# Two row blocks of the modulation weights per visit, accumulated in PSUM, in a two-layer DiT kernel

## Chip, core and metric

The kernel runs on one core of a Trainium2 chip. The metric is device time in microseconds (us) of one execution, start to end. TensorE is called PE, its weight loads PEld, VectorE DVE, ScalarE ACT, GpSimd POOL, and SP is the engine from whose queue nearly all loads are issued.

## The reference

Two layers of a diffusion transformer act on 512 latent tokens (stream `l`) and 256 context tokens (stream `c`) of width 1024. Each layer starts from six modulation rows per stream, which are one matrix product of a single vector with a wide weight matrix; the change concerns this product alone.

```python
silu_c = jax.nn.silu(c)
silu_cc = jax.nn.silu(c_ctx)
for l in range(DEPTH):
    mod_l = (silu_c @ w_mod[l] + b_mod[l])[:, None, :]       # w_mod[l]: 1024 x 6144
    mod_c = (silu_cc @ w_mod[l] + b_mod[l])[None, None, :]
    sh1, sc1, g1, sh2, sc2, g2 = jnp.split(mod_l, 6, axis=-1)
    h_l = modulate(rms_norm(x, norm1_g[l]), sh1, sc1)
    y_l, y_c = token_mixer(h_l, h_c, w_in[l], ...)           # projections, retention, attention, w_out
    x = x + g1 * y_l
    h_l = modulate(rms_norm(x, norm2_g[l]), sh2, sc2)
    x = x + g2 * expert_choice_ffn(h_l, ...)                 # 16 experts, top-k tokens
```

All arithmetic is float32; the projections split each operand into a high and a low part and add three products.

## The kernel before

**Stages.** Layer 0 first forms the modulation columns that it needs at once (`mod_half`), then projects both streams through `w_in` (some 50 to 410 us of the profile), multiplies by `w_out`, selects tokens and runs the experts, whose weights stream through a ring of 2 MB buffers (to about 1045 us). Layer 1 repeats this.

**Projections.** `proj` makes one projection of 256 output columns in eight steps (row blocks of 128). A tile `wraw` (512 KB) holds the weights of four steps, so a projection has two loads (L359), one before step 1 and one before step 5. Every two steps ACT copies half of `wraw` into `wH` (L275) and DVE or POOL subtracts to get `wL` (L276); there are two buffers of each. Then come 18 matmuls per step into `acc`: L354 and L355 read `wH`, L356 reads `wL`.

**Modulation.** `mod_gen` walks over 2048 columns at a time, row block by row block. One visit for one row block loads two tiles `wm` of 512 KB (L197), does four matmuls of 32 columns of weights side by side on PE (L201, one for each quarter of PSUM tile `ps_mod`), and DVE adds `ps_mod` to the running sum `modt` (L203). There are 40 visits in the stage: 16 for layer 0 and 24, made ahead, for layer 1.

**One set of buffers.** `wraw`, `wm` and later `wraw_o` (the weights of `w_out`, L866) share four buffers under the tag `wraw` (`NW = 4`). They are handed out in rotation, so a load may start when the tile four places earlier in the order of allocation has been read for the last time. SP issues its loads in order: behind one that waits, all wait.

**Order.** `weave` runs a projection step by step and after every step advances the attention by 0.8, the retention by 1.0 and the modulation by `M0R = 0.6` visits; after the last projection the rate of the modulation is `M1R = 0.5`. The counter starts anew with every projection, so visits come after steps 2, 4, 5 and 7. Within such an order the program's scheduler may move instructions of one engine past each other where their data allow it; on the chip each engine then works strictly in the order written.

Of the kernel before, what the change touches and what calls it, by code (L numbers as in the profile page):

```python
# [22 lines left out]
F32 = mybir.dt.float32  # L23
# [33 lines left out]
M0R, M1R = 0.6, 0.5  # L57
ATR, RTR, RTR2 = (0.8, 0.85), (1.0, 1.0), 0.7
# [12 lines left out]
def weave(main, *fills):  # L71

    acc = [0.0] * len(fills)
    for _ in main:
        for i, (g, r) in enumerate(fills):
            acc[i] += r
            while acc[i] >= 1.0:
                acc[i] -= 1.0
                next(g, None)
    return  # L80
# [9 lines left out]
def kernel(ctx_stack: ExitStack, tc: tile.TileContext, x, c, ctx, c_ctx, w_mod, b_mod, norm1_g,  # L90
# [4 lines left out]
    PE, ACT, DVE, POOL, SP = nc.tensor, nc.scalar, nc.vector, nc.gpsimd, nc.sync  # L95
# [50 lines left out]
    cT = cst.tile([128, KC, 32], F32, name="cT")  # L146
# [39 lines left out]
    def mod_gen(l, wp, pp, groups):  # L186

        for b in groups:
            m = wp.tile([128, 512], F32, name="modt", tag="modt", bufs=2)
            POOL.memset(m, 0.0)  # L190
            for r in range(2):
                POOL.dma_start(m[r:128:32], b_mod[l, 2048 * b:2048 * b + 2048].rearrange("(q n) -> q n", n=512))
            for k in range(KC):
                w = []
                for h in range(2):
                    w.append(wp.tile([128, 2, 512], F32, name="wm", tag="wraw", bufs=NW))
                    SP.dma_start(w[h], w_mod[l, 128 * k:128 * k + 128, 2048 * b + 1024 * h:2048 * b + 1024 * h + 1024]  # L197
                                 .rearrange("p (q n) -> p q n", q=2))
                ps = pp.tile([128, 512], F32, name="ps_mod", tag="t", bufs=4)
                for q in range(4):  # L200
                    PE.matmul(ps[32 * q:32 * q + 32], cT[:, k, :], w[q // 2][:, q % 2, :], start=True, stop=True,  # L201
                              tile_position=(0, 32 * q))
                DVE.tensor_add(m, m, ps)  # L203
                if k == KC - 1:
                    if b:
                        for r in range(2):
                            POOL.dma_start(mod_d[l][b][r].rearrange("(q n) -> q n", n=512), m[r:128:32])
                    mod_cols(l, b, m, pp)
                yield

    def mod_half(wp, pp, hf):

        m = wp.tile([128, 512], F32, name="modt", tag="modt", bufs=2)
        POOL.memset(m, 0.0)
        for r in range(2):
            POOL.dma_start(m[r:64:32], b_mod[0, 0:2048].rearrange("(q n) -> q n", q=2)[:, 512 * hf:512 * hf + 512])
        for k in range(0, KC, 2):
            ps = pp.tile([128, 512], F32, name="ps_mod", tag="t", bufs=4)
            for i in range(2):
                w = wp.tile([128, 2, 512], F32, name="wm", tag="wraw", bufs=NW)  # L220
                SP.dma_start(w, w_mod[0, 128 * (k + i):128 * (k + i) + 128, 0:2048]
                             .rearrange("p (q n) -> p q n", q=2)[:, :, 512 * hf:512 * hf + 512])
                for q in range(2):
                    g = 32 * (2 * i + q)
                    PE.matmul(ps[g:g + 32], cT[:, k + i, :], w[:, q, :], start=True, stop=True, tile_position=(0, g))
            DVE.tensor_add(m, m, ps)
            if k < KC - 2:
                yield
        ps = pp.tile([128, 4, 4, 32], F32, name="ps_mc", tag="t", bufs=4)
        for j in range(4):  # L230
            PE.transpose(ps[:, j].rearrange("p q r -> p (q r)"), m[:, 128 * j:128 * j + 128], ident)
        cs = slice(4 * hf, 4 * hf + 4)
        tmp = m[:, 0:32].rearrange("p (q s r) -> p q s r", q=4, r=2)
        DVE.tensor_copy(tmp, ps[:, :, :, 0:2].rearrange("p s q r -> p q s r"))
        DVE.tensor_tensor(tmp[:, 0:2], tmp[:, 0:2], tmp[:, 2:4], OP.add)
        for r in range(2):
            DVE.tensor_copy(B1[0][r][:, cs], tmp[:, 0, :, r])
            DVE.scalar_tensor_tensor(A1[0][r][:, cs], tmp[:, 1, :, r], 1.0, n1col[0][:, cs], op0=OP.add, op1=OP.mult)
        yield

    def mod_cols(l, b, m, pp):
        ps = pp.tile([128, 4, 4, 32], F32, name="ps_mc", tag="t", bufs=4)
        for s in range(4):
            PE.transpose(ps[:, s].rearrange("p q r -> p (q r)"), m[:, s::4] if b else m[:, 128 * s:128 * s + 128], ident)
        for r in range(2):
            v = ps[:, :, :, r].rearrange("p s q -> p q s")

            def o(t):
                return t[l][r].rearrange("p (q s) -> p q s", q=2)

            def g(t):
                return t[l].rearrange("p (q s) -> p q s", q=2)
            if b == 0:
                DVE.tensor_copy(o(B1), v[:, 0:2])
                DVE.scalar_tensor_tensor(o(A1), v[:, 2:4], 1.0, g(n1col), op0=OP.add, op1=OP.mult)
            elif b == 1:
                DVE.tensor_copy(o(B2), v[:, 2:4])
            else:
                DVE.scalar_tensor_tensor(o(A2), v[:, 0:2], 1.0, g(n2col), op0=OP.add, op1=OP.mult)
# [701 lines left out]
    def router_cols(l, streams, pp, R):  # L961

        for s in streams:
            ri = RI[s]
            R.wrA[s] = rp.tile([128, KC, 32], F32, name="wrA" + s)
            POOL.memset(R.wrA[s], 0.0)
            POOL.tensor_tensor(R.wrA[s][:, :, :16], R.wr, A2[l][ri][:, :, None].to_broadcast([128, KC, 16]), OP.mult)
            ps = pp.tile([128, 512], F32, name="ps_r", tag="t", bufs=4)[:, :16]
            for j in range(KC):
                PE.matmul(ps, B2[l][ri][:, j:j + 1].to_broadcast([128, 128]), R.wr[:, j, :], start=(j == 0),  # L970
                          stop=(j == KC - 1))
            R.bB[s] = rp.tile([128, 16], F32, name="bB" + s)
            DVE.tensor_copy(R.bB[s], ps)
            yield
# [539 lines left out]
    for l in range(2):  # L1514
# [3 lines left out]
        if True:  # L1518
# [18 lines left out]
            with ExitStack() as s2:  # L1537
                pp = s2.enter_context(tc.tile_pool(name=f"pp{l}", bufs=1, space=PSUM))
                m0 = router_cols(l, streams, pp, R) if l else None
                if l == 0:  # L1540
# [10 lines left out]
                    ps = pp.tile([128, 512], F32, name="ps_t", tag="t", bufs=4)  # L1551
# [8 lines left out]
                    m0 = mod_half(wq, pp, 0)  # L1560
# [11 lines left out]
                    m0 = chain(mod_gen(0, wq, pp, range(1, 3)), router_cols(0, streams, pp, R), mod_gen(1, wq, pp, range(0, 3)))  # L1572
# [11 lines left out]
                pj = projections(l, p, wq, pp, S, st, need)  # L1584
# [26 lines left out]
                with ExitStack() as s3:  # L1611
                    w = s3.enter_context(tc.tile_pool(name=f"mx{l}", bufs=1, side="left"))
                    Sp = w.tile([128, 6, 2, 2, 64], F32, name="Sp")

                    def ret_all():
                        while "rv" not in ready:
                            yield
                        for s in "cl":
                            yield from ret_states(s, p, pp, S[s], T, Sp)
                        ready.add("states")  # L1620
                        while not {"rq", "g0", "g1"} <= ready:
                            yield
                        for s in reversed(streams):
                            yield from ret_gen(s, w, p, pp, S[s], T, Sp)

                    at = attn_all(streams, w, p, pp, S, T, ready, st)
                    rt = ret_all()
                    runs.update(at0=at, states=rt)
                    for n in ORDER[l:]:
                        ss = "lc" if two or n in ("rk", "rv") else "l"  # L1630
                        weave(pj[n](ss), (at, ATR[l]), (rt, RTR[l]), (m0, M0R))
                        later.append(lambda n=n: ready.add(n))
                        if l and n == "rv":
                            ring.load(N0)
                    while later:
                        later.pop(0)()
                    weave(at, (rt, RTR2), (m0, M1R))
                    drain(rt, m0)
            p_s.close()
            ml_s, po_s, pc_s = ExitStack(), ExitStack(), ExitStack()  # L1640
# [40 lines left out]
            with ExitStack() as s2:  # L1681
                if not two:
                    p = po_s.enter_context(tc.tile_pool(name=f"po{l}", bufs=1, side="left"))
                pp = s2.enter_context(tc.tile_pool(name=f"pq{l}", bufs=1, space=PSUM))
# [134 lines left out]
            with ExitStack() as s2:  # L1819
                pp = s2.enter_context(tc.tile_pool(name=f"pe{l}", bufs=1, space=PSUM))  # L1820
# [85 lines left out]
```

## Time and profile before

| What | Value |
|---|---|
| median of 3 runs | 1892.11 us (1891.56 to 1894.91) |
| profiled execution, its own time | 1889.7 us |
| its span in the profile | 1887.9 us |
| PE busy | 1770.4 us (94%) |
| DVE, ACT, POOL busy | 655.8, 479.8, 329.9 us |
| issue to landing, median: `wm`, `wraw`, `wraw_o` | 4.6, 3.9, 4.1 us |

The span is 1.8 us shorter than that execution's own time. Busy means that at least one instruction of the engine was under way. PE is busy nearly all the time in the projections and in the experts, so a microsecond in which PE stands still there is a microsecond of the run unless something later makes up for it.

### The profile page before, as it was taken

Reading aid. Unit: us, or ns where it says so; the run is one execution under the profiler, and the core shown is the slowest. Engines: PE = TensorE matmul, PEld = TensorE weight load, DVE = VectorE, ACT = ScalarE, POOL = GpSimd, SP = SyncE. Lnnn points to the kernel's source line nnn. Section 1 sums busy time; section 2 is a strip of 40 time slices with the busy share of each in tenths; the row PEclk is TensorE's granted clock in tenths of the full one; section 3 lists DMA queues with packets and bytes.
Section 4 is the critical chain, followed back from the end, with each engine's and each line's share of the span. In section 5 each row is a group of like instructions: output and inputs, shape, how many; then the busy total and the mean of one; then the engine's idle time right before and its main releaser. Section 6 shows DMA issues by size and latency. Waiting matters only on the chain. (4 is left out here: it accounts for less than half of the span.)

```text
span 1887.9 us, 30047 instructions
## 1 busy us (share of the span) xinstructions
PE 1770.4 (94%) x12581; PEld 1018.5 (54%) x12581; DVE 655.8 (35%) x1671; ACT 479.8 (25%) x960; POOL 329.9 (17%) x341
## 2 busy tenths in 40 slices
PE   5899999999899999999999789899959999999995
PEld 2788877767533333333333688877745444534442
DVE  5645435673621001110001755446341122221224
ACT  3435434353411001010000446454331000000001
POOL 3323123333201011011001333322410000000001
PEclk9999999999899999999999899999979999999998
DMA  8454354257789999999998411111747999999995
GB/s 278 155 191 157 106 202 151 90 186 279 300 340 408 414 401 401 423 400 399 395 412 325 169 43 37 57 34 38 297 185 291 420 430 429 429 429 428 431 428 206
DMA packets 88919, 528.42 MB, mean 280 GB/s; under 512 B 9352, under 2 KB 31932, under 8 KB 64720
## 3 DMA queue, kind: packets, MB, share of 16 engines
q1 hardware_dynamic: 83040, 511.24, 68.0%
q0 software_dynamic: 5744, 15.26, 2.9%
q8 instruction: 99, 1.62, 0.3%
q14 instruction: 36, 0.29, 0.0%
HBM read 510.41 MB, written 16.06 MB: 279 GB/s over the span
## 5 line engine op out<-in xcount | busy, mean ns | idle before, releaser
L1133 PE MATMUL ps_g<-ring,xTl 128*32 128x512 f32 (+1 forms) x1472 | 238.0, 596 | 4.2 <-DMA ring<-in_w_gate_dram 3.0
L1133 PE MATMUL ps_u<-ring,xTl 128*32 128x512 f32 (+1 forms) x1536 | 233.1, 592 | 3.1 <-DMA ring<-in_w_up_dram 2.4
L1133 PE MATMUL ps_d<-ring,aT 128*32 128x512 f32 (+1 forms) x1536 | 234.6, 593 | 0.3 <-ACT sil L1241 0.3
L1270 ACT ACTIVATE aT<-ps_t 128x512 f32<-128x512 f32 x16 | 9.6, 598 | 619.0 <-PE ps_t L1266 578.1
L354 PE MATMUL acc<-wH,hHl 128*128 128x256 f32 x512 | 153.8, 301 | 2.7 <-ACT hHl L343 1.2
L1133 PEld LDWEIGHTS ps_g<-ring,xTl 128*32 128x32 f32 (+1 forms) x1472 | 72.7, 121 | 154.1 <-issue 137.5
L1133 PEld LDWEIGHTS ps_u<-ring,xTl 128*32 128x32 f32 (+1 forms) x1536 | 69.9, 119 | 153.1 <-issue 146.0
L355 PE MATMUL acc<-wH,hLl 128*128 128x256 f32 x512 | 147.0, 287 | 3.5 <-DVE hLl L344 3.4
L356 PE MATMUL acc<-wL,hHl 128*128 128x256 f32 x512 | 147.1, 287 | 1.1 <-DVE wL L276 1.1
L1133 PEld LDWEIGHTS ps_d<-ring,aT 128*32 128x32 f32 (+1 forms) x1536 | 70.4, 119 | 142.5 <-issue 136.7
L354 PEld LDWEIGHTS acc<-wH,hHl 128*128 128x128 f32 x512 | 99.7, 195 | 30.3 <-issue 23.7
L276 POOL TENSOR_TENSOR wL<-wraw,wH 128x512 fp32r<-128x512 f32 x44 | 57.5, 1308 | 275.0 <-ACT wH L275 263.8
L355 PEld LDWEIGHTS acc<-wH,hLl 128*128 128x128 f32 x512 | 99.8, 195 | 4.4 <-DVE hLl L344 4.4
L356 PEld LDWEIGHTS acc<-wL,hHl 128*128 128x128 f32 x512 | 99.8, 195 | 4.0 <-DVE wL L276 2.4
L1268 DVE COPY aT<-ps_t 128x512 f32<-128x512 f32 x16 | 11.1, 692 | 253.2 <-PE ps_t L1266 253.2
L1249 DVE TENSOR_TENSOR sil<-ps_u,sil 128x512 f32<-128x512 f32 x32 | 22.1, 692 | 220.8 <-PE ps_u L1133 220.8
L1185 POOL TENSOR_TENSOR x<-z,xTl 128x512 f32<-128x512 f32 x3 | 5.1, 1717 | 493.4 <-DVE x L1187 493.4
L678 DVE TENSOR_REDUCE mc<-ps_s 128x1 f32<-128x513 f32 (+2 forms) x80 | 55.2, 690 | 83.3 <-PE ps_s L675 52.1
L275 ACT ACTIVATE wH<-wraw 128x512 fp32r<-128x512 f32 x88 | 55.1, 629 | 95.6 <-PE acc L355 44.9
L680 ACT ACTIVATE P<-ps_s,mc 128x513 f32<-128x513 f32 (+2 forms) x80 | 55.1, 689 | 94.5 <-DVE mc L678 94.5
L1123 PE MATMUL ps_x<-OT,xn 128*128 128x128 f32 x512 | 67.0, 297 | 8.1 <-DVE OT L1115 8.1
L1123 PEld LDWEIGHTS ps_x<-OT,xn 128*128 128x128 f32 x512 | 65.3, 210 | 10.0 <-DVE OT L1115 8.5
(491 smaller groups left out, 3172.0 us busy)
## 6 DMA issues: line engine op xcount, KB each, us to landing
ring<-in_w_up_dram SPq DMA_DIRECT2D x62, 2048.0 KB, 16.6
ring<-in_w_gate_dram SPq DMA_DIRECT2D x61, 2048.0 KB, 13.3
ring<-in_w_down_dram SPq DMA_DIRECT2D x61, 2048.0 KB, 17.0
wm<-in_w_mod_dram SPq DMA_DIRECT2D x96, 512.0 KB, 4.6
wraw<-in_w_in_dram SPq DMA_DIRECT2D x44, 512.0 KB, 3.9
wraw_o<-in_w_out_dram SPq DMA_DIRECT2D x24, 512.0 KB, 4.1
ring<-in_w_gate_dram SPq DMA_DIRECT2D x12, 512.0 KB, 4.8
ring<-in_w_down_dram SPq DMA_DIRECT2D x12, 512.0 KB, 15.6
```

The costliest lines, as they stand in the source:

```text
L275: ACT.activation(H, src, AF.Copy)
L276: sub_eng().tensor_sub(L, src, f32(H))
L354: PE.matmul(ps, aH, bH, start=start, stop=False)
L355: PE.matmul(ps, aL, bH, start=False, stop=False)
L356: PE.matmul(ps, aH, bL, start=False, stop=stop)
L678: DVE.tensor_reduce(mc[:, 0:1], sc, AX.X, OP.max, negate=True)
L680: ACT.activation(P[:, :nk + 1], sc, AF.Exp, bias=mc[:, 0:1], accum_out=mc[:, 1:2])
L1123: PE.matmul(ps[:, j], R.xn[:, t, c0:c0 + 128], OT[:, t], start=(t == 0), stop=(t == 3))
L1133: PE.matmul(G[h][c:c + n], lhs[:, k, c:c + n], W[e][:, j, 512 * h:512 * h + 512], start=(k == 0), stop=(k == KC - 1), tile_position=(0, c))
L1249: DVE.tensor_mul(sil[p][:, hs], U[h], sil[p][:, hs])
L1268: DVE.tensor_copy(aT[p][:, 4 * h:4 * h + 4], ps)
L1270: ACT.activation(aT[p][:, 4 * h:4 * h + 4], ps, AF.Copy)
```

## The change

A visit now covers two row blocks: it loads four tiles `wm`, does eight matmuls, of which the second four are added to the first in PSUM, and DVE makes one addition. The rates of the modulation in `weave` are halved, so that as many row blocks are done per projection step; by the counter, visits now come after steps 4 and 7 of a projection.

```diff
             for k in range(KC):
                 w = []
+                if k % 2 == 0:
+                    ps = pp.tile([128, 512], F32, name="ps_mod", tag="t", bufs=4)
+                    both = []
                 for h in range(2):
                     w.append(wp.tile([128, 2, 512], F32, name="wm", tag="wraw", bufs=NW))
                     SP.dma_start(w[h], w_mod[l, 128 * k:128 * k + 128, 2048 * b + 1024 * h:2048 * b + 1024 * h + 1024]
                                  .rearrange("p (q n) -> p q n", q=2))
-                ps = pp.tile([128, 512], F32, name="ps_mod", tag="t", bufs=4)
-                for q in range(4):
-                    PE.matmul(ps[32 * q:32 * q + 32], cT[:, k, :], w[q // 2][:, q % 2, :], start=True, stop=True,
-                              tile_position=(0, 32 * q))
+                both.append(w)
+                if k % 2 == 0:
+                    continue
+                for i in range(2):
+                    for q in range(4):
+                        PE.matmul(ps[32 * q:32 * q + 32], cT[:, k - 1 + i, :], both[i][q // 2][:, q % 2, :],
+                                  start=i == 0, stop=i == 1, tile_position=(0, 32 * q))
                 DVE.tensor_add(m, m, ps)
...
-                        weave(pj[n](ss), (at, ATR[l]), (rt, RTR[l]), (m0, M0R))
+                        weave(pj[n](ss), (at, ATR[l]), (rt, RTR[l]), (m0, M0R / 2))
...
-                    weave(at, (rt, RTR2), (m0, M1R))
+                    weave(at, (rt, RTR2), (m0, M1R / 2))
```

**In the middle of a projection.** The first place is the queue of SP around `wraw_934` of before, the second load of the first projection with visits; in the change this load is `wraw_932`. This is SP before:

```order
L359 DMA wraw_793<-in_w_in_dram 128x4x256
L197 DMA wm_852<-in_w_mod_dram 128x1024
L197 DMA wm_854<-in_w_mod_dram 128x1024
L197 DMA wm_924<-in_w_mod_dram 128x1024
L197 DMA wm_926<-in_w_mod_dram 128x1024
L359 DMA wraw_934<-in_w_in_dram 128x4x256
```

And this is SP in the change, with the line numbers of the changed file:

```order
L365 DMA wraw_793<-in_w_in_dram 128x4x256
L200 DMA wm_915<-in_w_mod_dram 128x1024
L200 DMA wm_917<-in_w_mod_dram 128x1024
L200 DMA wm_919<-in_w_mod_dram 128x1024
L200 DMA wm_921<-in_w_mod_dram 128x1024
L365 DMA wraw_932<-in_w_in_dram 128x4x256
```

The order of the loads is the same in both; in both the second `wraw` takes the buffer of the first of the four `wm` ahead of it (852, and now 915).

PE at the same place before: the visit that reads `wm_924` and `wm_926`, and then step 5 of the projection, whose `wH_936` and `wL_937` are made from `wraw_934`. The visit that reads `wm_852` stands two steps earlier.

```order
L562 MATMUL ps_t_919<-ident_66,kl_709 128x128 x2
L201 MATMUL ps_mod_928<-wm_924,cT_106 32x512 x2
L201 MATMUL ps_mod_928<-wm_926,cT_106 32x512 x2
L354 MATMUL acc_799<-wH_936,hHl_350 128x256
L355 MATMUL acc_799<-wH_936,hLl_351 128x256
L356 MATMUL acc_799<-wL_937,hHl_350 128x256
```

PE there in the change (`wH_934` and `wL_935` are made from `wraw_932`):

```order
L568 MATMUL ps_t_905<-ident_66,kl_709 128x128 x2
L207 MATMUL ps_mod_914<-wm_915,cT_106 32x512 x2
L207 MATMUL ps_mod_914<-wm_917,cT_106 32x512 x2
L207 MATMUL ps_mod_914<-wm_919,cT_106 32x512 x2
L207 MATMUL ps_mod_914<-wm_921,cT_106 32x512 x2
L360 MATMUL acc_799<-wH_934,hHl_350 128x256
L361 MATMUL acc_799<-wH_934,hLl_351 128x256
L360 MATMUL acc_812<-wH_934,hHc_352 128x256
L362 MATMUL acc_799<-wL_935,hHl_350 128x256
```

The visit that frees the buffer of the load has moved from two steps ahead of its use to directly ahead of it.

**At the end of the stage.** The second place is SP where the last `wm` are followed by the first loads of `w_out` (`wraw_o`), a modulation row (`g1`) and the residual (`x`, 2 MB). Before:

```order
L197 DMA wm_4514<-in_w_mod_dram 128x1024
L197 DMA wm_4516<-in_w_mod_dram 128x1024
L197 DMA wm_4559<-in_w_mod_dram 128x1024
L197 DMA wm_4561<-in_w_mod_dram 128x1024
L866 DMA wraw_o_4636<-in_w_out_dram 128x2x512
L866 DMA wraw_o_4689<-in_w_out_dram 128x2x512
```

And in the change:

```order
L200 DMA wm_4537<-in_w_mod_dram 128x1024
L200 DMA wm_4539<-in_w_mod_dram 128x1024
L200 DMA wm_4541<-in_w_mod_dram 128x1024
L200 DMA wm_4543<-in_w_mod_dram 128x1024
L872 DMA wraw_o_4596<-in_w_out_dram 128x2x512
L270 DMA g1_4582<-mod01_109 128x1024
L1704 DMA x_4583<-in_x_dram 128x2x1024 x2
L872 DMA wraw_o_4649<-in_w_out_dram 128x2x512
```

On PE the last visit, which reads `wm_4537` to `wm_4543`, now stands behind the last matmuls of the attention and directly ahead of the `w_out` product; the first `wraw_o` takes the buffer of `wm_4537`, and `g1` and `x` have moved ahead of the second `wraw_o`.

## Rows read from the trace of the kernel before

**Rows 1.** The head of the page: the profiled span.

```profile
span 1887.9 us, 30047 instructions
```

**Rows 2.** Busy time by stretch: PE, PEld, DVE, ACT, POOL, clock, DMA share, GB/s.

```profile
100.00:400.00 300.00, 298.73 (x2254) 234.46 (x2253) 154.94 (x438) 124.26 (x256) 81.28 (x89) 1.00 0.45 150
600.00:1000.00 400.00, 397.99 (x3668) 130.48 (x3664) 43.01 (x73) 26.05 (x58) 41.99 (x31) 1.00 1.01 404
```

**Rows 3.** Instructions on tile ps_mod: count, duration min/median/max in ns.

```profile
L203 DVE TENSOR_TENSOR modt<-modt,ps_mod x40: 674/687/690, 76.4 to 407.3; 128x512 f32<-128x512 f32 x40
```

**Rows 4.** Timeline of PE around one visit: start us, us, instruction.

```profile
84.85 0.28 PE L356 MATMUL acc<-wL,hHc 128*128 128x256 f32 x1
85.06 1.07 PE L201 MATMUL ps_mod<-wm,cT 128*32 128x512 f32 x8
86.06 0.39 PE L354 MATMUL acc<-wH,hHl 128*128 128x256 f32 x1
86.28 0.28 PE L355 MATMUL acc<-wH,hLl 128*128 128x256 f32 x1
86.40 0.28 PE L356 MATMUL acc<-wL,hHl 128*128 128x256 f32 x1
```

**Rows 5.** Timeline of SP, 84 to 143 us: three issues of projection weights.

```profile
86.16 0.38 SPq L359 DMA_DIRECT2D wraw<-in_w_in_dram  x1
...
124.13 0.38 SPq L359 DMA_DIRECT2D wraw<-in_w_in_dram  x1
...
138.40 0.38 SPq L359 DMA_DIRECT2D wraw<-in_w_in_dram  x1
```

**Rows 6.** Timeline of ACT: the splits that waited for these three loads.

```profile
90.53 0.63 ACT L275 ACTIVATE wH<-wraw 128x512 fp32r<-128x512 f32 x1 [2.32 <-DMA wraw<-in_w_in_dram]
...
127.99 0.63 ACT L275 ACTIVATE wH<-wraw 128x512 fp32r<-128x512 f32 x1 [0.49 <-DMA wraw<-in_w_in_dram]
...
142.39 0.64 ACT L275 ACTIVATE wH<-wraw 128x512 fp32r<-128x512 f32 x1 [0.40 <-DMA wraw<-in_w_in_dram]
```

**Rows 7.** Instructions on tile wraw, and its loads from issue to landing.

```profile
L276 POOL TENSOR_TENSOR wL<-wraw,wH x44: 1263/1291/1594, 34.5 to 1318.3; 128x512 fp32r<-128x512 f32 x44
L276 DVE TENSOR_TENSOR wL<-wraw,wH x44: 675/692/1608, 36.0 to 1313.3; 128x512 fp32r<-128x512 f32 x44
...
DMA to landing us min/median/max: 3.5/3.9/6.8
```

**Rows 8.** Tile wm: its loads from issue to landing.

```profile
DMA to landing us min/median/max: 3.5/4.6/5.8
```

**Rows 9.** Waits of the SP queue, 71 to 413 us, the longest in total.

```profile
SPq L359 <- PE ps_mod L201: 107.3, 18, 12.3
```

**Rows 10.** Timeline of PE where the stage ends.

```profile
406.12 1.07 PE L201 MATMUL ps_mod<-wm,cT 128*32 128x512 f32 x8
...
408.85 1.15 PE L698 MATMUL ps_t<-ident,P 128*128 128x128 f32 x8
409.92 1.08 PE L711 MATMUL ps_o<-PT,avc 128*64 128x256 f32 x8
410.84 1.03 PE L711 MATMUL ps_o<-PT,avl 128*64 128x256 f32 x8
412.87 0.50 PE L354 MATMUL acc<-wH,mHl 128*128 128x512 f32 x1 [1.00 <-ACT mHl L275]
```

**Rows 11.** Timeline of SP there.

```profile
403.88 7.67 SPq L866 DMA_DIRECT2D wraw_o<-in_w_out_dram  x5
```

**Rows 12.** PE busy, granted clock, DMA share and GB/s around pauses of PE.

```profile
1201.60:1204.36 2.76, 0.73 (x6) 1.00 0.57 188
1204.36:1207.77 3.41, 3.12 (x16) 0.50 0.00 0
...
1827.50:1829.90 2.40, 0.01 (x2) 1.00 0.99 423
1829.90:1833.30 3.40, 3.40 (x16) 1.00 0.97 414
```

## The prediction

> **What bounds it now.** I began with the busy shares by stretch. From 100 to 400 us, in which most of the 40 visits lie, PE is busy 298.73 of 300 us, DVE 154.94, ACT 124.26, POOL 81.28, and the DMA engines 45% [rows 1, 2]: the stage is bound by the row of work on PE. So one addition less per pair on DVE gives nothing by itself; 20 additions of 0.687 us, 13.7 us [rows 3], go from an engine that is idle half the time. Behind this stage come the experts, where PE and the DMA engines are both full (share 1.01, 404 GB/s) [rows 2]; their transfers start only after it, so what the stage loses or gains reaches the end of the run in full.
>
> Next I looked at what the PE work waits for. The queue of SP waited 18 times, 107.3 us in all, for `ps_mod` before a projection load could start [rows 9]: the visits free the buffers of the projection weights. The visit that begins at 85.06 is followed by the issue at 86.16, 1.1 later [rows 4, 5]; this distance is 1.07 to 1.09 for all 18. The load issued at 86.16 is split by ACT from 90.53, those of 124.13 and 138.40 from 127.99 and 142.39: 4.37, 3.86 and 3.99, mean 4.07, and in all three ACT was waiting for the load [rows 5, 6]. The split takes 0.63, the subtraction on DVE 0.69 [rows 6, 7]. So, counted from the start of the visit that frees the buffer, `wH` is ready at 1.1 + 4.07 + 0.63 + some 0.07 for two hand-overs = 5.87 us, and `wL` 0.73 later, at 6.60. Before, every such load has another whole visit and at least one step of 18 matmuls between the two, and PE hardly ever waits.
>
> **The change, part by part.**
>
> *Work of PE.* The eight matmuls of a pair do the same passes as twice four. Removed is one entry into the narrow weights and one exit per pair. Between 84.85 and 85.06 lie 0.21 instead of the 0.12 that such a matmul takes (86.28 to 86.40), and the first matmul behind the visit takes 0.22 instead of 0.12 (86.06 to 86.28) [rows 4]: 0.09 + 0.10, times 20 visits saved, is 3.8, say -4 us. The visit itself lasts 1.0 (85.06 to 86.06), a double one 2.0. The Trainium skill, "TensorEngine Tiling (Array Packing)", Key Properties, says that changing the tiling mode drains TensorE; the trace agrees, with these 0.1 us on either side.
>
> *The loads of projection weights.* This is where the change costs. In the order of SP nothing moves, and each `wraw` still takes the buffer of the first `wm` ahead of it. But that `wm` now belongs to a visit four tiles long which stands directly ahead of the step that needs the load (after step 4), or one step ahead (after step 7). So the wait of [rows 9] ends a whole visit later, and the 5.87 us must be covered by the double visit (2.0) and by what the new order puts between it and the first use. I took the order of PE in the changed kernel, and priced what stands between: 0.12 per matmul of 256 columns [rows 4], 0.13 per transpose, 0.12 per value product [rows 10]. For the place shown above it is nothing: 2.0 us of cover for 5.87, and 2.35 for the 6.60 of `wL`, so PE stands still for 4.25. There are 19 such loads; two, beside the router's two turns without visits, have 18 us of cover and more. For the other 17, in order, cover up to the first use of `wH`: 2.0, 4.1, 2.5, 4.8, 2.7, 5.2, 4.2, 5.8, 2.0, 4.1, 4.9, 5.5, 4.1, 5.4, 4.9, 6.1, 4.9. The stall is the greater of 5.87 less this and 6.60 less the cover of `wL`: 4.3, 1.8, 3.7, 1.0, 3.4, 0.7, 1.8, 0.1, 4.1, 1.8, 1.2, 0.4, 2.2, 0.5, 1.1, 0.4, 1.2. Sum: **29.7 us**. What is queued behind the waiting matmul is all of PE, the attention included; ACT waits at its split, with the attention's exponentials behind it.
>
> The bounds: with the quickest landing, 3.5 against the median 3.9 [rows 7], every stall is 0.4 shorter, some 6 less (24). With landings of 4.6, as the `wm` loads have when several run at once [rows 8], it is 0.7 more each, 41. I take the middle since three other loads follow the load at once in both kernels.
>
> *The fourth `wm` of a visit after step 7* takes the buffer of the `wraw` loaded in mid-projection. It starts after the second half is split, POOL's 1.29 included [rows 7], and lands 4.6 later [rows 8]: 1.1 + 4.07 + 0.63 + 0.63 + 1.29 + 0.3 + 4.6 = 12.6 after the earlier visit began, 13 to 14 where POOL or ACT is held up. The shortest distance in the order is 9.8 of work plus the stall of 3.4 to 4.3, plus 1.5 inside the visit: 14 to 15. I take +1, between 0 and 5.
>
> *The end of the stage.* Before, the last visit starts at 406.12, the first `wraw_o` is issued at 403.88, and PE loses only 1.00 ahead of the `w_out` product [rows 10, 11]. In the change the last two visits have 18 transposes and value products between them (2.3 us), and the four loads of the last wait for the one before: first landing 1.1 + 4.6 after its start, the fourth later by three times 512 KB at the 404 GB/s of [rows 2], 3.9: some 3.4 of stall. Then the first `wraw_o` waits for the last visit (5.87 against 2.0 plus the addition and four transposes): 1 to 2 us, in place of the 1.00. And `g1` and `x`, 2.5 MB or 6 us of transfer, now stand ahead of the second `wraw_o`: up to 2. Together **+6**, between +2 and +9.
>
> *The clock.* A pause of PE has a second price. From 1201.60 to 1204.36 PE was busy 0.73 of 2.76 us, and for the next 3.41 us the granted clock was 0.50, the 1.2 GHz level: 1.7 us lost. After an idle 1827.50 to 1829.90 it stayed 1.00 [rows 12]. I went through all pauses of PE in the timeline: of the six over 2 us five were followed by the low clock, of those from 1.3 to 1.9 some one in three. Of my stalls five are over 2 us, three are 1.8, one or two lie at the end: 7 or 8 falls of 1.7 to 2, **+13**, between 0 and +22.
>
> *Layer 1* has only the router's columns on this rate; they move from step 2 to step 4: nothing, hidden by PE's own work.
>
> **Sum.** -4 + 29.7 + 1 + 6 + 13 = +45.7. The profiled execution took 1889.7, which gives 1935.4; the median of the runs is 2.4 above it, so on that scale about **1937**.
>
> **Rivals.**
>
> 1. *The stalls come, but the clock holds*, as after 1829.90: +33, 1925. Against it: five of six.
> 2. *The loads land later* than the mean, because a projection load and three `wm` now start within 1.5 us of each other, or ACT, held at its splits, delays the attention which I counted as cover. Landings of 6.8, the longest [rows 7], are 2.9 over the median; on 12 of the 17 loads that is 35 more: 1960 and above. For it: landing times do spread from 3.5 to 6.8; against it: the load is first in its queue.
> 3. *The loads are hidden anyway*, within 0.2% (3.8 us, about what a measurement of this kernel can tell from no change): the order finds cover. Against it: it is written out, and twelve of the 17 places have under 5 us of cover. The Trainium skill, "Perfetto Trace Analysis", Identifying Performance Opportunities, reads a gap that repeats on the engine that should be full as a sign of too few buffers; this trace shows no such gap yet, and by that rule the change would make one.
> 4. *Faster.* The deciding point is a cover of 5.87 us at each use. If the split could start 4 us sooner (the buffer free before the visit), only the removed entries and exits remain, -4, and at most the 13.7 of DVE where it stands on the path: 1874 to 1888. For it: DVE's work shrinks; against it: [rows 9] say that the buffer is what is waited for.
>
> **Chances.** The forecast, stalls with falls of the clock (1929 to 1950): 0.60. Rival 1 or a smaller sum (1912 to 1929): 0.20. Rival 2 (1950 and above): 0.15. Rival 3: 0.02. Rival 4: 0.03. The low end is -4 + 24 + 0 + 2 + 0 = +22, 1914; the high end -4 + 41 + 3 + 8 + 20 = +68, 1960. Between them lie more than 8 in 10. Slower by over 0.2%: 0.95, within 0.2%: 0.02, faster: 0.03.
>
> **What would show it.** In the profile after, from 70 to 420 us: waits of PE or its weight loads at L360 or L362 for ACT's `wH` or DVE's `wL`, some 25 to 40 us in all, three to four of about 4 us where the visit is followed at once by step 5; ACT waiting longer for `wraw` than before; PE below 90% busy where it was 99.6%; granted clock below 1.00 in some of the 50 us stretches; the first `w_out` matmul at about 458 instead of 412.87; 20 additions in place of 40; and after that stage everything as before, only later. I am wrong if the loads are issued other than 1.1 us after their visit, if they land in much less than 4, or if PE pauses at other work.

## The result, and the profile after the change

The change made the kernel slower: 1956.13 us median (1952.9 to 1957.71, 4 runs) against 1891.84 of the kernel before on the same chip (1888.8 to 1894.91, 4 runs). The ratio is 1.0341, 95% interval 1.0325 to 1.0358. I had forecast 1937, in a range from 1914 to 1960: the direction is right and the place for the most part, the size is 19 us short.

The profiled execution took 1955.45 us. The first thing to settle is where the 65.8 us between the two profiled times were lost. The first rows here are the first projection matmul, before and after (timelines of PE; columns are start, duration, instruction, and in brackets the idle time ahead and what ended it):

```profile
33.94 0.38 PE L354 MATMUL acc<-wH,hHl 128*128 128x256 f32 x1 [1.20 <-ACT wH L275]
```

```profile
36.82 0.39 PE L360 MATMUL acc<-wH,hHl 128*128 128x256 f32 x1 [1.20 <-ACT wH L281]
```

The next view of the kernel after the change is the timeline of PE where the stage ends, which answers to [rows 10]:

```profile
469.12 2.00 PE L207 MATMUL ps_mod<-wm,cT 128*32 128x512 f32 x8
471.50 1.05 PE L207 MATMUL ps_mod<-wm,cT 128*32 128x512 f32 x4 [0.38 <-DMA wm<-in_w_mod_dram]
472.79 1.05 PE L207 MATMUL ps_mod<-wm,cT 128*32 128x512 f32 x4 [0.23 <-DMA wm<-in_w_mod_dram]
475.59 0.75 PE L250 MATMUL ps_mc<-ident,modt 128*128 128x128 f32 x4 [1.75 <-DVE modt L209]
477.05 0.47 PE L360 MATMUL acc<-wH,mHl 128*128 128x512 f32 x1 [0.70 <-DVE A21c L265]
```

The first `w_out` matmul moved from 412.87 [rows 10] to 477.05, 64.2 later, so nearly all of the loss lies ahead of it. Of this, 2.9 lie ahead of the projections, where the change touches nothing; in the executions profiled below this start lies between 33.7 and 37.8 whatever the kernel. From the first projection matmul to the first `w_out` matmul it was 378.93 before and is 440.23 now: +61.3. These are the busy times by stretch, first that whole stretch of before, and then of the kernel after the change the same stretch, the two stretches of [rows 2], and three pieces of 50 us (columns: from and to, length, busy time of PE, PEld, DVE, ACT and POOL with the number of instructions, granted clock, DMA share, GB/s):

```profile
33.94:412.87 378.93, 369.93 (x2792) 291.19 (x2792) 206.04 (x565) 160.01 (x337) 104.14 (x117) 0.99 0.46 154
```

```profile
36.82:477.05 440.23, 394.31 (x2793) 311.30 (x2793) 200.07 (x551) 165.80 (x355) 107.28 (x122) 0.94 0.38 131
100.00:400.00 300.00, 274.32 (x2031) 222.15 (x2024) 119.43 (x334) 110.94 (x233) 70.61 (x77) 0.97 0.39 136
600.00:1000.00 400.00, 397.86 (x3656) 132.95 (x3652) 47.08 (x86) 33.71 (x75) 39.53 (x31) 1.00 1.00 406
...
100.00:150.00 50.00, 42.57 (x322) 37.04 (x315) 19.27 (x55) 16.75 (x41) 13.14 (x14) 0.93 0.45 159
200.00:250.00 50.00, 49.63 (x411) 42.25 (x411) 21.24 (x56) 24.12 (x43) 9.09 (x11) 1.00 0.23 76
400.00:450.00 50.00, 46.52 (x255) 34.03 (x257) 27.54 (x90) 14.61 (x27) 13.46 (x15) 0.83 0.15 53
```

The experts (600 to 1000) are as full as before. In the projections the number of matmuls is the same (2793 against 2792), but PE is idle 45.9 us (440.23 - 394.31) instead of 9.0, and it is busy 24.4 us longer with the same work. The granted clock shows in what way: below 1.00 in most pieces, 1.00 from 200 to 250, where the router's turns leave no visits and PE is busy 49.63 of 50 us as it was before.

What PE waited for in the kernel after the change, 60 to 480 us (total, number, longest):

```profile
PE acc L360 <- ACT wH L281: 21.8, 13, 7.0
PE ps_s L672 <- DVE mc L689: 6.6, 4, 2.7
PE ps_u L766 <- POOL vw L761: 2.3, 1, 2.3
PE ps_mc L250 <- DVE modt L209: 1.8, 1, 1.8
PE acc L362 <- DVE wL L282: 1.3, 1, 1.3
...
PE acc L361 <- DVE wL L282: 0.9, 1, 0.9
```

Before, the longest wait of PE in this stretch was 1.81 us. Now it waits above all for `wH`, 13 times. The SP queue's wait for `ps_mod`, which [rows 9] put at 107.3 us in 18 waits, has grown with the same count:

```profile
SPq L365 <- PE ps_mod L207: 203.4, 18, 39.9
```

From the first visit to the end of the stage the granted clock fell seven times; before, it did not fall between 61 and 413 us. Four of the seven stretches, and the sum over all seven:

```profile
85.20:95.40 10.20, 6.24 (x29) 6.23 (x30) 1.36 (x3) 4.34 (x12) 1.27 (x1) 0.50 0.47 180
122.70:126.10 3.40, 3.40 (x17) 3.21 (x17) 0.37 (x3) 0.90 (x3) 1.27 (x1) 0.50 0.79 270
...
266.10:272.90 6.80, 4.78 (x22) 4.79 (x23) 0.69 (x1) 1.15 (x2) 1.28 (x1) 0.50 0.87 328
...
412.80:429.90 17.10, 15.06 (x61) 12.17 (x62) 5.28 (x16) 5.54 (x10) 4.69 (x5) 0.50 0.00 0
sum 47.70, PE 39.50 PEld 35.65 DVE 7.97 ACT 12.94 POOL 18.40; mean PE 5.64 PEld 5.09 DVE 1.14 ACT 1.85 POOL 2.63
```

At 0.50, the 1.2 GHz level, half of the busy time is lost: 39.50 / 2 = 19.8 us, an estimate. Ahead of the visits each kernel has one more low stretch, with 5.95 us of busy PE before and 3.24 now, which makes 1.4 less. So the 61.3 us are +36.9 of idle time (45.9 - 9.0), about +18.4 of clock, and some 6 that show as longer busy time of the same matmuls (24.4 - 18.4). These 6 are pauses as well. The record of a matmul lasts longer than the step to the next one, so the last record ahead of a pause covers its beginning: in these rows L681 starts 0.07 after L679, yet the records last 0.23 and 0.22, and the pause counts only from 411.70 on.

```profile
411.41 0.23 PE L679 MATMUL ps_s<-mprev,identb 128*128 128x128 bf16 x1
411.48 0.22 PE L681 MATMUL ps_s<-mnext,identb 128*128 128x128 bf16 x1
414.36 0.58 PE L672 MATMUL ps_s<-akHc,q 128*128 128x256 f32 x1 [2.66 <-DVE mc L689]
```

At the full clock 13 matmuls of this stretch stand directly ahead of a pause before, and 44 now. Their records exceed the mean step of undisturbed matmuls of the same form by 2.5 us and by 9.3 us in all: some +6.8 of hidden pauses, an estimate from the records of the two traces.

The pause in these rows is also the one in front of the longest fall of the clock (412.8 to 429.9), and PE does not wait for a load there. The last projection load was issued at 388.32, the double visits next to it start at 387.23 and 432.18, and what PE waits for is DVE's work on earlier scores of the attention (`mc`). The 2.66 us and half of the 15.06 us of busy PE at the low clock make some 10 of the 61.3 us at this one place, an estimate.

### The profile page after: what moved, and what is told of

The parts are those of the page before. It is cut to its first block, busy times and chain, and to the rows that moved or that the text cites. A ratio compares the mean times of both kernels' runs of the same rounds, so it can differ in the third digit from the quotient of the medians.

```text
span 1953.7 us, 29998 instructions
## 1 busy us (share of the span) xinstructions
PE 1802.8 (92%) x12581; PEld 1044.6 (53%) x12581; DVE 642.8 (33%) x1651; ACT 479.1 (25%) x960; POOL 327.5 (17%) x341
## 5 line engine op out<-in xcount | busy, mean ns | idle before, releaser
L362 PE MATMUL acc<-wL,hHl 128*128 128x256 f32 x512 | 151.5, 296 | 2.7 <-DVE wL L282 2.4
L281 ACT ACTIVATE wH<-wraw 128x512 fp32r<-128x512 f32 x88 | 54.0, 627 | 58.8 <-PE acc L361 37.8
```

The costliest lines, as they stand in the source:

```text
L281: ACT.activation(H, src, AF.Copy)
L362: PE.matmul(ps, aH, bL, start=False, stop=stop)
```

## The experiments

Three theories were set against each other. **Theory 1**, that of the prediction: the projection loads take buffers that the visit directly ahead frees, and PE waits for the load, and then works at the low clock. **Theory 2**: the accumulation, or the one late addition for both, costs. **Theory 3**: the length of a double visit costs, since PE is held in one piece. Ratios are to the kernel before, run on the same chip.

### e1: the accumulation alone

Single visits at the old rates and places; two share a PSUM tile and one addition.

```diff
-                ps = pp.tile([128, 512], F32, name="ps_mod", tag="t", bufs=4)
+                if k % 2 == 0:
+                    ps = pp.tile([128, 512], F32, name="ps_mod", tag="t", bufs=4)
                 for q in range(4):
                     PE.matmul(ps[32 * q:32 * q + 32], cT[:, k, :], w[q // 2][:, q % 2, :],
-                              start=True, stop=True, tile_position=(0, 32 * q))
+                              start=k % 2 == 0, stop=k % 2 == 1, tile_position=(0, 32 * q))
+                if k % 2 == 0:
+                    yield
+                    continue
                 DVE.tensor_add(m, m, ps)
```

> The accumulation alone: two visits of one row block each, at the old rates and in the old places, share one PSUM tile, and DVE makes one addition for both. Theory 1 (shared buffers: the change loses because the four loads of a pair stand directly ahead of the projection step whose load takes one of their buffers): by the order there are stalls of 1.5 us in all at the mid-projection loads, against 2.0 before and 30.7 in the change, so the time is that of before, 1886 to 1896 us, with 20 additions. Theory 2 (accumulation: an accumulation left open in PSUM, or one addition for both, late, is what costs): 1920 us or more. Theory 3 (length: a double visit holds PE for 1.85 us in one piece, and attention and splits wait for it): as before, since the visits are single ones.

Measured: 1894.67 us, ratio 1.0012 (1.0003 to 1.0021). There is next to no effect; what there is has the wrong sign for a gain. There are 20 additions. PE is as busy as before in the stretch of [rows 2] (298.60 against 298.73 us), and DVE is 15 us lighter:

```profile
100.00:400.00 300.00, 298.60 (x2223) 231.32 (x2221) 139.71 (x406) 122.35 (x251) 80.49 (x89) 1.00 0.44 147
```

So the accumulation and the missing additions are worth nothing by themselves, and theory 2 falls.

### e2: the pairing alone

```diff
-                    ps = pp.tile([128, 512], F32, name="ps_mod", tag="t", bufs=4)
...
                 for i in range(2):
+                    ps = pp.tile([128, 512], F32, name="ps_mod", tag="t", bufs=4)
                     for q in range(4):
                         PE.matmul(ps[32 * q:32 * q + 32], cT[:, k - 1 + i, :], both[i][q // 2][:, q % 2, :],
-                                  start=i == 0, stop=i == 1, tile_position=(0, 32 * q))
-                DVE.tensor_add(m, m, ps)
+                                  start=True, stop=True, tile_position=(0, 32 * q))
+                    DVE.tensor_add(m, m, ps)
```

> The pairing alone: visits of two row blocks at the halved rates, as in the change, but each row block has its own PSUM tile and its own addition (40 additions). Theory 1 (shared buffers): stalls of 30.4 us by the order, so as slow as the change: 1945 to 1965 us. Theory 2 (accumulation and the one addition cost): near before, 1890 to 1910. Theory 3 (length): as slow as the change.

Measured: 1951.43 us, ratio 1.0315 (1.0295 to 1.0335). With 40 additions and no accumulation nearly the whole loss is there, and the same wait leads the list:

```profile
PE acc L360 <- ACT wH L281: 17.3, 11, 4.2
```

The loss comes from the pairing of the visits and their loads. This does not yet tell theory 1 from theory 3.

### e3: a buffer of their own for the projection loads, and e7, its control

```diff
-NP = 6
+NP = 5
...
-            m = wp.tile([128, 512], F32, name="modt", tag="modt", bufs=2)
+            m = wp.tile([128, 512], F32, name="modt", tag="modt", bufs=1)
...
-                raw = wq.tile([128, 4, 256], F32, name="wraw", tag="wraw", bufs=NW)
+                own = (w, "praw", 1) if l == 0 else (wq, "wraw", NW)
+                raw = own[0].tile([128, 4, 256], F32, name="wraw", tag=own[1], bufs=own[2])
```

> The change, but the projection loads of layer 0 have one buffer of their own, so that none waits for a visit; to make room, the attention's P tiles have 5 buffers instead of 6 and the running sum one instead of two. Visits, order and accumulation stay as in the change. Theory 1 (shared buffers): the stalls go and the clock with them: 1885 to 1900 us, the first w_out matmul near 413, no waits of PE for wH over 1.5 us at these places. Theory 2 (accumulation) and theory 3 (length): the loss stays, 1940 or more. If it lies between, at 1905 to 1940, the buffers are a part and the rest is something else, or the smaller pools cost, which a run of the kernel before with the same smaller pools will tell.

Measured: 1899.61 us, ratio 1.0041 (1.0026 to 1.0056), with the double visits and their accumulation as in the change. PE has no wait for `wH` among its longest; these lead the list now, 60 to 424 us:

```profile
PE ps_mod L207 <- issue: 1.9, 1, 1.9
PE ps_t L580 <- DVE q L601: 1.8, 2, 0.9
PE ps_mod L207 <- DMA wm<-in_w_mod_dram: 1.8, 4, 0.9
```

The same own buffer and smaller pools in the kernel before (e7) tell what they cost by themselves.

> Control: the kernel before with what the own buffer needed and brought (projection loads of layer 0 in one buffer of their own, 5 buffers of P, one running sum). It stalls hardly at all before, so nothing is to gain from the buffer. If the smaller pools and the single own buffer are what left the change with its own buffer 0.4% above before: 1895 to 1903 us. If the change itself costs that much still: as before, 1888 to 1895.

Measured: 1896.97 us, ratio 1.0032 (1.0018 to 1.0046). The intervals of e3 and e7 overlap: with the shared buffers out of the way, the change costs nothing that these runs can tell. Theory 3 falls, and theory 1 stands with most of the 3.4%. One thing did not stay as in the change: PE's order. Of the 2792 matmuls of the stage, 2434 can be matched in sequence, by the tiles they write and read, with those of the change (2768 in e10 below, which alters only the end). The pause of 414.36 is gone in e3 too, although PE waits for no load there. It stands in all the runs that keep the change's order (e2, e8, e9 and e10, 2.46 to 2.66 us) and in none with another (e3 to e6). Whether late loads or the order alone bring it and its 10 us, no run here tells.

### e4, e5, e6: the double visits at other steps

The counter of `weave` starts ahead, so that the same double visits come after steps 3 and 7 (0.15), 2 and 6 (0.4), or 2 and 5 (0.55) instead of 4 and 7. No buffer is added.

```diff
-def weave(main, *fills):
+def weave(main, *fills, ahead=0.0):
 
-    acc = [0.0] * len(fills)
+    acc = [0.0] * (len(fills) - 1) + [ahead]
...
-                        weave(pj[n](ss), (at, ATR[l]), (rt, RTR[l]), (m0, M0R / 2))
+                        weave(pj[n](ss), (at, ATR[l]), (rt, RTR[l]), (m0, M0R / 2), ahead=0.15)
```

> The change with the modulation's counter started at 0.15 in each projection, so that the double visits come after steps 3 and 7 instead of 4 and 7: one more step of 18 matmuls stands between the visit that frees the buffer and the first use of the load. Theory 1 (shared buffers): stalls of 11.2 us by the order instead of 30.7, so some 20 less, and of the 20 us that the low clock costs half or more come back: 1915 to 1938 us; the two gaps of 7.0 and 4.1 us in the timeline of PE shrink to about 3 and 1 or go. Theories 2 and 3 (accumulation, length): the same number of double visits and additions, so as the change, 1950 or more.

> The change with the modulation's counter started at 0.4 in each projection: the double visits come after steps 2 and 6, so that two whole steps of 18 matmuls stand between the visit that frees a buffer and the first use of the load that takes it. Theory 1 (shared buffers): by the order the stalls are 1.2 us in all instead of 30.7, so the loss of the stage goes nearly whole: 1886 to 1900 us, no low clock before the last step of the stage. What could be left: the fourth load of the visit after step 6 takes the buffer of the load used in steps 5 to 8 and may land late, 1 or 2 us per projection, which would show as waits of the visits for wm and give 1900 to 1915. Theories 2 and 3 (accumulation, length of a visit) are already spoken against; they would leave it at 1940 or more.

> The same with the counter started at 0.55: double visits after steps 2 and 5. Theory 1 (shared buffers): stalls of 1.0 us by the order, 1886 to 1900 us; if the late fourth load of the visit after step 6 or 5 is the next wait, this kernel, in which that load has one step less, is the slower of the two by some us, with more waits of the visits for wm.

Measured: 1932.74 (ratio 1.0213, 1.0198 to 1.0229), 1905.94 (1.0077, 1.0064 to 1.0090) and 1904.50 us (1.0069, 1.0051 to 1.0088). The stalls that I had worked out from the order fall as 30.7 (the change; the sum of the prediction was 29.7), 11.2, 1.2 and 1.0 us, and the loss falls with them as 3.4, 2.1, 0.8 and 0.7%. In e4 PE still waits 10.7 us for `wH` and `wL`:

```profile
PE acc L360 <- ACT wH L281: 6.4, 9, 1.9
PE acc L361 <- DVE wL L282: 4.3, 2, 3.4
```

In e6 these are gone from the head of the list, and the clock is back to 0.99:

```profile
PE ps_u L766 <- POOL vw L761: 3.3, 2, 3.1
PE ps_mod L207 <- DMA wm<-in_w_mod_dram: 2.3, 3, 1.3
```

```profile
100.00:400.00 300.00, 294.76 (x2210) 233.81 (x2198) 139.77 (x412) 123.34 (x252) 80.41 (x89) 0.99 0.40 140
```

My expectation that e6 would be slower than e5, since its late `wm` has a step less, was wrong: their intervals overlap and the waits for `wm` are equal, 2.3 us. Both stay 13 to 15 us above before, by their ratios, and so above the 1886 to 1900 that I had given for theory 1. In the profiles this loss lies in the stage: from the first projection matmul to the first `w_out` matmul it is 391.19 in e5 and 392.84 in e6 against 378.93, and PE is idle 19.6 and 17.0 us of it against 9.0. Single waits of 2 to 3 us each stand in the list; why they come is open.

### e8 and e9: work for PE in three of the pauses

This asks for the clock alone. The loads stay as late as they are, but PE does not stand still while it waits.

```diff
+FILL = {1: 48, 3: 10, 9: 30}
...
                 DVE.tensor_add(m, m, ps)
+                visit[0] += 1
+                if visit[0] in FILL:
+                    ps = pp.tile([128, 512], F32, name="ps_fill", tag="t", bufs=4)
+                    for i in range(FILL[visit[0]]):
+                        PE.matmul(ps[:, :128], ident, ident, start=True, stop=True)
```

> The change with PE kept at work in three of its longest pauses: directly behind the 1st, 3rd and 9th double visit stand 48, 10 and 30 matmuls of 128 columns on the identity, 6.3, 1.3 and 3.9 us at 0.13 each, whose results are not read (this is work added, nothing is left out). The loads and their waits are as in the change, so no load comes earlier. If the clock falls because PE pauses: the low stretches at 85 (10.2 us), 122 (3.4) and 266 us (6.8) go, some 20 us at half speed, and the time falls by 6 to 10 us, to 1944 to 1951, although nothing was taken away. If the clock falls for another reason: the low stretches stay and the time is that of the change or some us more, 1955 to 1962.

Measured: 1953.43 us, ratio 1.0337 (1.0319 to 1.0354), between the two expectations. The clock no longer falls behind the three filled visits; this stretch, at 0.93 in the change, is at 1.00 in e8:

```profile
100.00:150.00 50.00, 44.78 (x366) 38.20 (x366) 20.02 (x58) 18.65 (x45) 13.18 (x14) 1.00 0.45 159
```

But the filling was too long and ate what the clock gave back. So I ran it again with 22, 6 and 18 matmuls.

> As e8, but sized by what e8 showed: one matmul of the filling takes 0.223 us (two passes), not 0.13, so that its 48, 10 and 30 took 10.7, 2.3 and 6.7 us and stood past the end of the pauses by some 8 us. Now 22, 6 and 18 of them, 4.9, 1.3 and 4.0 us, behind the same three visits (work is added, nothing left out). If the clock falls because PE pauses: the low stretches at 85, 122 and 266 us stay away as in e8, and without the 8 us of overrun the time is 1943 to 1949 us. If the filling only moves the time about: 1952 to 1958.

Measured: 1946.57 us, ratio 1.0290 (1.0267 to 1.0313). Work was added and the time fell by 9.6 us against the change (1956.13 to 1946.57; the intervals of the two ratios do not meet). The timelines of PE show it at the two places where the low clock went. At the third, behind the third visit, it came all the same (121.4 to 124.8), against my expectation. In the change, from the first double visit to the second, and from the ninth to the tenth:

```profile
80.25 1.92 PE L207 MATMUL ps_mod<-wm,cT 128*32 128x512 f32 x16 [0.89 <-PE ps_t L568]
89.16 0.58 PE L360 MATMUL acc<-wH,hHl 128*128 128x256 f32 x1 [6.99 <-ACT wH L281]
...
98.55 1.92 PE L207 MATMUL ps_mod<-wm,cT 128*32 128x512 f32 x16
...
262.04 1.92 PE L207 MATMUL ps_mod<-wm,cT 128*32 128x512 f32 x16
268.12 0.58 PE L360 MATMUL acc<-wH,hHl 128*128 128x256 f32 x1 [4.15 <-ACT wH L281]
...
276.81 1.92 PE L207 MATMUL ps_mod<-wm,cT 128*32 128x512 f32 x16
```

And in e9:

```profile
80.88 1.92 PE L210 MATMUL ps_mod<-wm,cT 128*32 128x512 f32 x16 [0.89 <-PE ps_t L576]
84.59 5.15 PE L217 MATMUL ps_fill<-ident 128*128 128x128 f32 x44 [1.79 <-DVE akLl L579]
89.80 0.39 PE L368 MATMUL acc<-wH,hHl 128*128 128x256 f32 x1
...
96.85 1.92 PE L210 MATMUL ps_mod<-wm,cT 128*32 128x512 f32 x16
...
261.58 1.92 PE L210 MATMUL ps_mod<-wm,cT 128*32 128x512 f32 x16
...
274.32 1.92 PE L210 MATMUL ps_mod<-wm,cT 128*32 128x512 f32 x16
```

The first matmul on `wH` comes 8.9 us after the visit's start in both (89.16 - 80.25 and 89.80 - 80.88): no load came sooner. Yet the next visit follows after 15.97 us instead of 18.30, and at the other place after 12.74 instead of 14.77, 4.4 us for the two. So the pauses at these places do bring the low clock, and a pause costs more than its length. The 9.6 us are not all owed to the filling: in the profiles the stage is 3.8 us shorter (436.40 against 440.23), and the rest of the difference lies ahead of it and behind it, where the edit touches nothing.

### e10 and e11: single visits at the end of the stage

Behind the last projection the visits are single again, as in e1, at the old rate; the rest is the change (e10), or e6 (e11).

```diff
-                if k % 2 == 0:
+                if k % 2 == 0 and not tail_[0]:
                     continue
-                for i in range(2):
+                for i in ((k % 2,) if tail_[0] else range(2)):
...
+                    tail_[0] = True
-                    weave(at, (rt, RTR2), (m0, M1R / 2))
+                    weave(at, (rt, RTR2), (m0, M1R))
```

> The change, but the visits behind the last projection are single row blocks again at the rate of before, two of them sharing one accumulation and one addition as in e1; in the projections everything is as in the change. This takes the end of the stage by itself: there the last double visit waited for its own loads (PE stood 0.38 and 0.23 with three loads behind it, and the visit took 6.47 us instead of 1.85). If the end of the stage costs what the prediction gave it, +6 (2 to 9): 1947 to 1954 us, and the last visits without a wait for wm of over 1 us. If the end costs nothing: 1955 to 1958.

> Double visits after steps 2 and 5, as in e6, and single ones behind the last projection, as in e10. Theory 1 (shared buffers): both places where the change waits are mended, what is left of e6's 0.7% are waits inside some visits for wm and the score and state matmuls: 1893 to 1901 us, at best level with before. It would be faster than before, 1885 to 1889, only if the entries saved on PE (some 5 us) were no longer eaten by waits.

Measured: e10 1951.32 us, ratio 1.0318 (1.0301 to 1.0334), 4.8 us below the change, but the intervals overlap; e11 1911.73, ratio 1.0104 (1.0087 to 1.0121), 7.2 us above e6, where I had expected a gain (their intervals just touch). The timeline of PE in e10, from the first of the last two visits, shows that what is won there is given back:

```profile
461.00 1.06 PE L209 MATMUL ps_mod<-wm,cT 128*32 128x512 f32 x8
...
466.97 0.77 PE L365 MATMUL acc<-wH,mHl 128*128 128x512 f32 x1 [1.21 <-DVE A21c L270]
...
476.53 0.50 PE L365 MATMUL acc<-wH,mHl 128*128 128x512 f32 x1 [2.31 <-ACT wH L286]
...
478.48 0.79 PE L367 MATMUL acc<-wL,mHl 128*128 128x512 f32 x1 [1.03 <-DVE wL L287]
```

From the start of the last two row blocks to the first `w_out` matmul it is 5.97 us (461.00 to 466.97), where the change takes 7.93 (469.12 to 477.05). But the second and later `wraw_o` stand behind `g1` and `x` in the queue, and the product then waits 2.31 and 1.03 us for them. From the start of the last two row blocks to the first matmul of the experts it is 110.5 us in e10 (461.0 to 571.5) against 106.9 in the change (469.1 to 576.0). So the trace does not place a gain at the end, and the 4.8 us are not explained by it; the profiled execution is the fastest of e10's five. In e11 the same two pauses (2.29 and 1.14) come, followed by 6.8 us of low clock. From the first `w_out` matmul to the first matmul of the experts it is 105.2 us (428.2 to 533.4) against 100.0 in e6 (427.4 to 527.4), while the stage ahead of it is no longer than in e6 (391.64 against 392.84): most of the difference lies at these pauses. No version tried beats the kernel before.

## Why the prediction was right in kind and short in size

**The loads: right.** The mechanism, the places and the count hold: 18 waits of SP for `ps_mod`, in front of loads that PE then waits for; with a buffer of their own (e3) the loss goes, and with a better place (e5, e6) most of it. The waits of PE for `wH` and `wL` sum to 24.0 us (21.8 + 1.3 + 0.9), where I gave 29.7 with 24 as the lower bound. At the ninth visit I had 4.1 and it is 4.15. At two of the four places of about 4 us the stall is broken up: part of it is a wait of the attention's scores for `mc` (1.53 us ahead of 120.12 and 1.23 ahead of 156.31), which stands in the cover and is late itself. The longest of the four waits for `mc` is another matter: the 2.66 us ahead of 414.36, at no load, for which the prediction has no term. So that the three terms which are idle time of PE, 29.7 + 1 + 6 = 36.7, came out as 36.9 is luck: less of it than forecast stands at the loads, more at other waits, and some 6.8 us of pauses hide in the busy time, so that the pauses come to 43.7.

At the first visit I had 4.25 and it is 6.99, for a reason that neither the sum nor a rival has: ACT is busy with tables when the load lands. These are the timelines of SP and of ACT there:

```profile
81.33 0.38 SPq L365 DMA_DIRECT2D wraw<-in_w_in_dram  x1
```

```profile
82.18 2.44 ACT L466 ACTIVATE tab<-jpf,lg 128x128 f32<-128x128 f32 x8 [3.38 <-DVE lg L455]
84.53 3.26 ACT L483 ACTIVATE qtab<-iq,lgq 64x128 f32<-64x128 f32 x8
...
88.49 1.14 ACT L281 ACTIVATE wH<-wraw 128x512 fp32r<-128x512 f32 x2
```

The issue comes 1.08 after the visit's start at 80.25, as forecast. With the median landing of 4.0 us the weights are there at 85.3, but ACT makes tables until 87.8 and, after three short instructions, splits at 88.49. Before, the split waited 2.32 us for the load [rows 6], so the load was late and not ACT. For the whole stage, too, my sign "ACT waits longer for `wraw`" was wrong: it waits 12.6 us in all, against 38.5 before. ACT waits for `mc` instead, 91.2 us against 61.8. Two more signs were narrowly missed: the waits of PE for `wH` and `wL` are 24.0 us and not 25 to 40, and PE is busy 91.4% from 100 to 400 us (274.32 of 300) and not below 90%.

**The clock: right in kind, mis-sized.** I gave +13, and about 18 came. The number of falls, seven, is what I gave (7 or 8). Their length is not: I priced every one at 1.7 to 2 us after one stretch of 3.41 us [rows 12], but three of them lasted 6.8, 10.2 and 17.1 us, the last with 15.06 us of busy PE, some 7.5 lost, behind a pause at no load. The trace of the kernel before held a longer fall than the one that I priced by: from 54.1 to 60.9, 6.8 us, behind a pause of 2.10 ahead of 54.95.

**Work of PE: right where undisturbed, and not seen in the sum.** A double visit without a wait takes 1.85 us (98.55 to 100.40) instead of twice 1.0 [rows 4], and one entry and exit are saved. But in place of the -4 that I gave, busy time apart from the clock rose by some 6. Without the hidden pauses (6.8) it came out about 1 us shorter, not 4. So the shortfall of the stage, 45.7 forecast and 61.3 come, is some 7 of pauses (43.7 against 36.7), 5 of the clock and 3 of this term.

**The fourth `wm`: nothing instead of +1.** No visit ahead of the last waited inside for a load. In e3, e5 and e6, without the stalls that hide it, the visits wait 1.8 to 2.3 us in all for `wm`.

**The end of the stage: +6 forecast, not borne out.** PE stands 3.1 us there (0.38 + 0.23 + 1.75 + 0.70) against 1.5 before (0.51 and 1.00), and from the first `w_out` matmul to the first matmul of the experts it is 98.9 us against 97.7: some 3 us. e10, which was to take the end by itself, does not settle it.

**The rivals.** Rival 1, that the clock holds, is refuted by e8 and e9. The time of 1956 lies in the band that I gave to rival 2 (1950 and above, 0.15) and not in that of the forecast (1929 to 1950, 0.60), though hardly by rival 2's way: landings moved only from 3.9 to 4.0 us. Its other half, late attention in the cover, is seen in the waits for `mc`; and ACT held at its tables, which it did not name, cost 2.7 us at one place. Rivals 3 and 4 are out by the result. The Trainium skill, "Perfetto Trace Analysis", Identifying Performance Opportunities, says that a gap repeating on the engine that should be full can mean too few buffers; the traces agree, since with one buffer more, for the projection loads alone (e3), the thirteen waits for `wH` are gone from the list.

## What to carry to other kernels

When two streams of loads share a rotation of buffers, grouping one stream's uses moves the release of a buffer closer to the use of the other stream's load: write down for each load which use frees its buffer and how much work lies between that and its own first use, since this sum told most of the places and most of the size here. Where the larger group is wanted, shift its place in the order before asking for memory: a start value of 0.4 in a counter took the loss from 3.4% to 0.8%. And price a pause of TensorE by more than its length, with a fall of the clock behind it that may last several times as long as the pause.

## What the runs showed of the hardware

- A pause of 2.66 us (411.70 to 414.36) came with 17.1 us at the 0.50 clock, 412.8 to 429.9, although PE was busy 15.06 of them. In e10 the same place had 16.72 us of busy PE in 17.1, 408.7 to 425.8, and the clock stayed at 0.50 all the same. Behind the pause of [rows 12] it was 3.41 us.
- Matmuls whose result nobody reads shortened the program: by 4.4 us at two places of the timeline; the medians fell by 9.6 us, of which the profiles place 3.8 in the stage.
- A 128x128 float32 matmul on the identity took 0.23 us each (22 of them, with two records each, 5.15 us in e9), not the 0.13 that I had from the transposes of the same size [rows 10]. That was the error in e8's sizing.
- The start of the projections moved between 33.7 and 37.8 us from one profiled execution to the next, whatever the kernel; differences of 3 us in a single profile are not read as effects.
